# Modulation sums in operations of 1024 columns, and another address for the last FFN's first-product operand

## The chip, the cores and the metric

The kernel runs on one core of a Trainium2 chip. The metric is the device time of one execution in microseconds (us). The kernel before took 1702.43 us, the median of three runs (1701.34 to 1703.19). The profile was taken in one more execution.

## The reference

Two layers of a diffusion transformer work on 256 latent tokens and 256 context tokens of width 1024, in float32. Each layer is a feed-forward network (FFN), a mixer (window attention and retention side by side) and a second FFN. Every sublayer takes a shift, a scale and a gate from a modulation vector:

```
mod   = silu(c)     @ ada_w[l] + ada_b[l]      # 9 x 1024 numbers per layer, latent stream
mod_c = silu(c_ctx) @ ada_w[l] + ada_b[l]      # the same for the context stream

u = rmsnorm(h, g_pre) * (1 + scale) + shift    # swiglu_sublayer
a, b = split(u @ wi);  y = (silu(a) * b) @ wo
h = h + 0.5 * gate * rmsnorm(y, g_post)
```

`wi` is 1024 x 5632 and `wo` 2816 x 1024. In the last layer the context stream ends at the mixer, so the last FFN has 256 tokens where the others have 512. `ada_w[l]` is 1024 x 9216; the product with it is a matrix by one vector per stream.

## The kernel before, in words

**Products.** TensorE (PE) takes operands rounded to fp32r. Each float32 operand is split into a high part and a rest, and a product is made of three matmuls: high by high, rest by high, high by rest. In the first product of an FFN (`uT`) the weights of 128 x 128 are the stationary operand, `whi` (L203, L204) or `wlo` (L205), and the activations `uh` and `ul` move through: 512 columns (two streams of 256), in the last FFN 256 columns. In the second product and in the mixer's output product the activations are stationary and 512 columns of weights move.

**Weights.** SyncE (SP) issues the loads in one queue: 512 KB into `raw` (five buffers). ScalarE (ACT) makes `whi` (L165) and VectorE (DVE) makes `wlo = raw - whi` (L166), 128 x 1024 at a time, with three buffers each. A step of an FFN's first product, `pair(f)`, takes two such weights and 48 matmuls, after which ACT and DVE make one gated tile `g` (L438, L439).

**Modulation.** The first two of the 18 modulation vectors come from PE at the start (`ada_slice`). The other 16 are summed on DVE, beside the FFNs' products: `ada_steps` runs in eight steps per vector. A step loads two half rows of 256 KB (`rawa`, three buffers, on SP's queue with the weights) and makes four operations of 512 columns (L284), each a product with `cbc` and a sum along the row into one column of `adacc`; the elementwise result goes to `junk` and is not read. After eight steps the two half sums are added (L289, `adav`) and `ada_done` makes the shift, scale or gate. `Filler` hands these steps out between the pairs of an FFN; they are bound by `start[0]` and `behind[0]` not to come before a given load and a given VectorE operation.

**Mixer.** In the retention part, `ret_out` makes the heads' outputs in `ps_ry`; ACT copies the second half (`y2`, L840) and DVE adds it (L841), then come the statistics on DVE, a power on GpSimd (POOL), and ACT scales each 128 x 128 tile with `rgn` (L855). `ret_T` transposes four of them on PE into `ps_ro` (L861), and ACT and DVE split that into `uh` and `ul` (L874) for the output product (`ps_wo`, L213 to L215). `y2` has one buffer of its own, `yr2`.

**Order.** The program is written as one list, and a scheduler puts each engine's instructions in an order from the operations' costs and from when buffers come free; this order is fixed when the kernel is built. The engines run each its own list and wait for one another by semaphores. Most short-lived tiles come from one pool of 26 slots of 2 KB per partition (`t2k`), which are handed round in the order of the requests.

**Addresses.** In the built kernel the tiles of `uh`, `ul`, `whi`, `wlo` and `w4` all begin at addresses that leave 160 when divided by 512 bytes, and so do all slices of them that a matmul of an FFN's first product reads.

Of the kernel before, what the change touches and what calls it, by code (L numbers as in the profile page):

```python
# [15 lines left out]
P = 128  # L16
L = 2
D = 1024
# [14 lines left out]
def hybrid_kernel(ctx: ExitStack, tc: tile.TileContext, A: dict, out: bass.AP):  # L33
# [18 lines left out]
    def small(shape, name, bufs=4):  # L52
        return t2.tile(shape, F32, tag=name, name=name, bufs=bufs)
# [18 lines left out]
    shT = const.tile([P, 3, 2, KT], F32, name="shT")  # L72
    scT = const.tile([P, 3, 2, KT], F32, name="scT")
    cbc = const.tile([P, 2, D], F32, name="cbc")
    ctile = const.tile([P, KT, 32], F32, name="ctile")

    def keep_warm(n):

# [11 lines left out]

    h = act.tile([P, 4, D], F32, name="h")

    uh = act.tile([P, 2, KT, LAT], R, name="uh")
    ul = act.tile([P, 2, KT, LAT], R, name="ul")

    c_in = small([P, KT, 2], "c_in", 1)
    nc.sync.dma_start(c_in, A["cT"])
# [100 lines left out]
    def uT(ps, w2, k, s0, s1):  # L198

        ps = ps.rearrange("p (s c) -> p s c", c=LAT)  # L200
        hi, lo = (w[:, k, :] for w in w2)
        mhi, mlo = (x[:, s0:s1, k, :] for x in (uh, ul))
        nc.tensor.matmul(ps, lhsT=hi, rhs=mhi, start=(k == 0), stop=False)  # L203
        nc.tensor.matmul(ps, lhsT=hi, rhs=mlo, start=False, stop=False)  # L204
        nc.tensor.matmul(ps, lhsT=lo, rhs=mhi, start=False, stop=(k == KT - 1))  # L205
# [15 lines left out]
    def ada_done(l, m, v):  # L221

        sub, kind = divmod(m, 3)
        for st in range(2):
            b = adab[:, l, m, :]
            if kind == 0:
                nc.vector.tensor_add(shT[:, sub, st, :], v[:, st, :], b)
            elif kind == 1:
                nc.vector.tensor_add(v[:, st, :], v[:, st, :], b)
                nc.vector.scalar_tensor_tensor(out=scT[:, sub, st, :], in0=v[:, st, :], scalar=1.0,  # L230
                                               in1=gpre[:, l, sub, :], op0=ALU.add, op1=ALU.mult)
            else:
                nc.vector.tensor_add(v[:, st, :], v[:, st, :], b)
                nc.vector.scalar_tensor_tensor(out=v[:, st, :], in0=v[:, st, :], scalar=(1.0 if sub == 1 else 0.5),
                                               in1=gpost[:, l, sub, :], op0=ALU.mult, op1=ALU.mult)
        if kind == 2:
            pt = psum([2 * KT, P], "ps_mt")
            nc.tensor.transpose(pt, v.rearrange("p s k -> p (s k)"), ident)
            row = small([2 * KT, P], "grow", 1)
            nc.vector.tensor_copy(row, pt)  # L240
            gd = dram.tile([2, D], F32, name=f"gd{l}{m}", tag=f"gd{l}{m}")
            nc.gpsimd.dma_start(gd.rearrange("s (k c) -> (s k) c", c=P), row)
            gdram[l, sub] = gd

    def ada_slice(j):


        ps = psum([P, 256], "ps_ada")
        for i in range(2):
            for m in range(2):  # L250
                wr = load_raw(A["ada_w0"][j, m, i], (4, 256))
                r = 64 * m + 32 * i
                for k in range(4):
                    nc.tensor.matmul(ps[r:r + 32, :], lhsT=ctile[:, 4 * i + k, :], rhs=wr[:, k, :], start=(k == 0),
                                     stop=(k == 3))
        mod = t2k([P, 256], name="mod")
        nc.scalar.activation(mod, ps, AF.Copy)
        pt = psum([P, 2, 2, 2], "ps_mt")
        for c2 in range(2):
            nc.tensor.matmul(pt[:, c2].rearrange("p m s -> p (m s)"), lhsT=mod[:, 128 * c2:128 * c2 + 128],  # L260
                             rhs=sel.rearrange("p m s -> p (m s)"), start=True, stop=True)
        ks = slice(2 * j, 2 * j + 2)
        v = small([P, 2, KT], "adav", 1)
        for st in range(2):
            nc.vector.tensor_add(shT[:, 0, st, ks], pt[:, :, 0, st], adab[:, 0, 0, ks])
            nc.vector.tensor_add(v[:, st, ks], pt[:, :, 1, st], adab[:, 0, 1, ks])
            nc.vector.scalar_tensor_tensor(out=scT[:, 0, st, ks], in0=v[:, st, ks], scalar=1.0,
                                           in1=gpre[:, 0, 0, ks], op0=ALU.add, op1=ALU.mult)
# [3 lines left out]

    def ada_steps(l, m):

        acc = small([P, 2, 2, KT], "adacc", 2)
        for k in range(KT):
            wr = [wp.tile([P, 512], F32, tag="rawa", name="rawa", bufs=3) for _ in range(2)]
            for i in range(2):
                with tc.issue_after(start[0]):
                    nc.sync.dma_start(wr[i], A["ada_w"][l, m, k, :, 512 * i:512 * i + 512])  # L280
                with tc.issue_after(behind[0]):
                    for st in range(2):
                        junk = small([P, 512], "junk", 2)
                        nc.vector.scalar_tensor_tensor(out=junk, in0=wr[i], scalar=1.0,  # L284
                                                       in1=cbc[:, st, 512 * i:512 * i + 512], op0=ALU.mult,
                                                       op1=ALU.mult, accum_out=acc[:, i, st, k:k + 1])
            yield
        v = small([P, 2, KT], "adav", 1)
        nc.vector.tensor_add(v, acc[:, 0], acc[:, 1])  # L289
        ada_done(l, m, v)  # L290

    class Filler:
# [72 lines left out]
    def pre_norm_part(sub, s, xn, k2):  # L365
        pt = psum([P, 2, 256], "ps_tr")
        for k in (0, 1):
            q, c0 = divmod(128 * (k2 + k), 512)
            for i in (0, 1):
                last = nc.tensor.transpose(pt[:, k, 128 * i:128 * i + 128], xn[i][q][:, c0:c0 + 128], ident)  # L370
        uf = t2k([P, 2, 256], name="uf")
        for k in (0, 1):
            sc, sh = scT[:, sub, s, k2 + k:k2 + k + 1], shT[:, sub, s, k2 + k:k2 + k + 1]
            nc.scalar.activation(uf[:, k, :], pt[:, k, :], AF.Identity, scale=sc, bias=sh)
        hi = uh[:, s, k2:k2 + 2, :]
        nc.vector.tensor_copy(hi, uf)  # L376
        behind[0] = nc.vector.tensor_sub(ul[:, s, k2:k2 + 2, :], uf, hi.bitcast(F32)).ins  # L377
        return last.ins

    def post_half(y, gates, t, half, part):  # L380


        junk = small([P, 512], "junk", 2)
        ss = small([P, 1], "ssy", 12)
        nc.scalar.activation(junk, y, AF.Square, scale=D ** -0.5, accum_out=ss)
        if half:
            st = small([P, 1], "ssum", 12)
            nc.vector.scalar_tensor_tensor(out=st, in0=part[0][0], scalar=RMS_EPS, in1=ss, op0=ALU.add, op1=ALU.add)
            ss = rsqrt(st)
        x = t2k([P, 512], name="x")  # L390
        nc.vector.tensor_mul(x, y, gates[t // 2][:, 512 * half:512 * half + 512])
        part[half] = ss, x
# [37 lines left out]
    def ffn(l, name, sub, streams, fill, nxt):  # L430
# [38 lines left out]
        def first_of_all():  # L469

            for t in range(4):
                pre_scale(t)
            t2.tile([P, 64], F32, name="pad3", tag="pad3", bufs=1)
            xn = [[xns.pop(2 * s), xns.pop(2 * s + 1)] for s in range(2)]
            gf = [t2k([P, n], name="g") for _ in range(2)]
            ps = [psum([P, n], "ps_up") for _ in range(4)]

            def norm(j):
                for s in range(2):
                    pre_norm_part(0, s, xn[s], 2 * j)  # L480

            def mm(j, f):
                for i in range(2 * f, 2 * f + 2):
                    for k in (2 * j, 2 * j + 1):
                        uT(ps[i], w[i], k, 0, 2)

            ada_slice(0)
            norm(0)
            w = [load(0, 0), load(0, 1), load(1, 0), load_w_4(wi[l, 3])]
            for j in range(4):  # L490
                mm(j, 0)
                if j < 3:
                    ada_slice(j + 1)
                    norm(j + 1)
                mm(j, 1)
            for f in range(2):
                gated(gf[f], *ps[2 * f:2 * f + 2])
            g.extend(gf)
# [59 lines left out]
    def mixer(l, last):  # L558
# [271 lines left out]
        def ret_out(hd):  # L830
            for s in range(streams):
# [4 lines left out]
                        nc.tensor.matmul(py[:, i], lhsT=pp[:, 128 * i:128 * i + 128], rhs=vr[kt][:, hd],  # L836
                                         start=(n_ == 0), stop=(n_ == len(both) - 1))
                y = small([P, 2, P], "yr", 4)
                y2 = small([P, 2, P], "yr2", 1)
                nc.scalar.activation(y2, py[:, :, 1, :], AF.Copy)  # L840
                nc.vector.tensor_add(y, py[:, :, 0, :], y2)  # L841
                st = small([P, 2, 6], "bst", 4)
# [83 lines left out]
        if last:  # L926
            for t in range(nt):
                for half in range(2):
                    mm(half, 3, t)
                    post_half(ys[half, t], gates, t, half, parts[t])  # L930
                post_norm(parts[t], t, 2)
                pre_scale(t)
                fill.step(1)
            keep_warm(12)
            pre_norm(2, 0)
            return
        fill.drain()
# [97 lines left out]
```

## Time and profile before

| what | value |
|---|---|
| median of three runs | 1702.43 us |
| the profiled execution, own time | 1700.97 us |
| its span (first to last instruction) | 1699.1 us |
| TensorE's granted clock, mean | 0.998 of full speed |
| PE busy | 98% of the span |
| DVE busy | 69% |
| ACT busy | 44% |
| POOL busy | 3% |

The profiled execution lies 1.46 us below the median. Its span is 1.9 us shorter than its own time, which is what lies around the first and last instruction. A busy PE is counted from modelled ends of its matmuls, which overlap, so the rate of a stretch is read from the distances between the starts of matmuls, not from their lengths. PEld is the loading of stationary operands. "Waits" lists, for an engine and line, the idle time that one releaser ended, with the number of times and the longest; the same wait can appear for PE and for PEld.

### The profile page before, as it was taken

How to read it: one execution, taken by the hardware profiler on the slowest of the kernel's cores; microseconds unless marked ns; L12 is line 12 of the kernel's file. 1: busy time of each engine (PE TensorE's matmuls, PEld its weight loads, DVE VectorE, ACT ScalarE, POOL GpSimd, SP SyncE). 2: the span in 40 equal slices, each digit the busy share in tenths (PEclk: the TensorE clock that was granted, in tenths of full speed). 3: DMA queues.
4: the chain of work that ended last, by engine and by line, in shares of the span. 5: the costliest groups of instructions: out<-in, count | busy, mean ns of one | idle time of the engine just before them, and what ended most of it. 6: DMA issues, size and time to landing. Idle time of an engine off the chain costs nothing.

```text
span 1699.1 us, 23653 instructions
## 1 busy us (share of the span) xinstructions
PE 1671.2 (98%) x8632; PEld 1408.6 (83%) x8632; DVE 1179.5 (69%) x2625; ACT 746.8 (44%) x1299; POOL 45.8 (3%) x75
## 2 busy tenths in 40 slices
PE   8999999999999999999999999999999999989998
PEld 5788788888778788888888898888888888889996
DVE  3699895496898869982245689962347589865466
ACT  4322222355787662222234452222234578754454
POOL 1000000001000110000000000000000100000000
PEclk9999999999999999999999999999999999999999
DMA  7677775252112236672333437752334222335563
GB/s 275 225 233 249 225 236 164 87 192 88 63 51 88 74 112 216 230 232 104 99 100 98 163 123 236 236 184 91 98 100 142 76 94 81 119 136 186 183 189 113
DMA packets 89270, 254.40 MB, mean 150 GB/s; under 512 B 10560, under 2 KB 11056, under 8 KB 89024
## 3 DMA queue, kind: packets, MB, share of 16 engines
q1 hardware_dynamic: 88416, 251.16, 45.0%
q0 software_dynamic: 736, 1.72, 0.3%
q8 instruction: 68, 1.11, 0.3%
q14 instruction: 50, 0.41, 0.1%
HBM read 251.74 MB, written 1.10 MB: 149 GB/s over the span
## 4 chain that ended last, share of the span: by engine, by line
PE 80%; DVE 7%; ACT 3%; DMA 3%; issue 2%; POOL 1%; DVEq 0%; POOLq 0%; ACTq 0%
PE ps_up L203 14%; PE ps_up L205 14%; PE ps_up L204 14%; PE ps_dn L535 8%; PE ps_dn L536 8%; PE ps_dn L537 8%; DMA rawa<-in_ada_w 3%; DVE junk L284 2%; DVE wlo L166 2%; PE ps_pj L203 1%; PE ps_pj L204 1%; PE ps_pk L213 1%; PE ps_pj L205 1%; PE ps_pk L215 1%; PE ps_po L693 1%
## 5 line engine op out<-in xcount | busy, mean ns | idle before, releaser
L165 ACT ACTIVATE whi<-raw 128x1024 fp32r<-128x1024 f32 x297 | 314.7, 1060 | 769.7 <-PE ps_up L204 499.0
L166 DVE TENSOR_TENSOR wlo<-raw,whi 128x1024 fp32r<-128x1024 f32 x297 | 362.9, 1222 | 284.5 <-ACT whi L165 279.6
L203 PE MATMUL ps_up<-uh,whi 128*128 128x512 f32 (+1 forms) x1400 | 502.1, 359 | 2.5 <-DVE uh L376 2.4
L205 PE MATMUL ps_up<-uh,wlo 128*128 128x512 f32 (+1 forms) x1400 | 502.3, 359 | 2.2 <-DVE wlo L166 2.1
L204 PE MATMUL ps_up<-ul,whi 128*128 128x512 f32 (+1 forms) x1400 | 501.8, 358 | 0.0
L284 DVE SCALAR_TENSOR_TENSOR junk<-rawa,cbc 128x512 f32<-128x512 f32 x512 | 325.8, 687 | 27.0 <-DMA rawa<-in_ada_w 26.3
L205 PEld LDWEIGHTS ps_up<-uh,wlo 128*128 128x128 f32 x1400 | 265.2, 189 | 43.7 <-DVE wlo L166 5.1
L203 PEld LDWEIGHTS ps_up<-uh,whi 128*128 128x128 f32 x1400 | 264.9, 189 | 42.7 <-DVE uh L376 3.8
L204 PEld LDWEIGHTS ps_up<-ul,whi 128*128 128x128 f32 x1400 | 265.3, 189 | 39.0 <-DVE ul L377 0.8
L537 PE MATMUL ps_dn<-wlo,ghl 128*128 128x512 f32 x560 | 217.9, 389 | 0.0
L536 PE MATMUL ps_dn<-whi,ghl 128*128 128x512 f32 x560 | 217.9, 389 | 0.0
L535 PE MATMUL ps_dn<-whi,ghl 128*128 128x512 f32 x560 | 216.9, 391 | 0.2
L535 PEld LDWEIGHTS ps_dn<-whi,ghl 128*128 128x128 f32 x560 | 104.6, 188 | 24.1 <-ACT ghl L525 3.0
L536 PEld LDWEIGHTS ps_dn<-whi,ghl 128*128 128x128 f32 x560 | 105.1, 188 | 22.3 <-DVE ghl L526 0.4
L537 PEld LDWEIGHTS ps_dn<-wlo,ghl 128*128 128x128 f32 x560 | 105.1, 188 | 21.9
L439 DVE TENSOR_TENSOR g<-g,ps_up 128x512 f32<-128x512 f32 (+1 forms) x92 | 55.0, 598 | 85.9 <-PE ps_up L205 79.7
L526 DVE TENSOR_TENSOR ghl<-g,ghl 128x512 fp32r<-128x512 f32 (+1 forms) x176 | 102.8, 619 | 1.4 <-ACT ghl L525 1.0
L525 ACT ACTIVATE ghl<-g 128x512 fp32r<-128x512 f32 (+1 forms) x176 | 92.1, 564 | 24.8 <-DVE g L439 15.9
L203 PE MATMUL ps_pj<-uh,whi 128*128 128x256 f32 (+1 forms) x168 | 58.7, 349 | 0.0
L204 PE MATMUL ps_pj<-ul,whi 128*128 128x256 f32 (+1 forms) x168 | 56.0, 333 | 0.1
L205 PE MATMUL ps_pj<-uh,wlo 128*128 128x256 f32 (+1 forms) x168 | 55.6, 331 | 0.0
L438 ACT ACTIVATE g<-ps_up 128x512 f32<-128x512 f32 (+1 forms) x92 | 47.0, 511 | 0.0
(220 smaller groups left out, 1958.9 us busy)
## 6 DMA issues: line engine op xcount, KB each, us to landing
raw<-in_ffn_wi SPq DMA_DIRECT2D x176, 512.0 KB, 3.8
rawa<-in_ada_w SPq DMA_DIRECT2D x256, 256.0 KB, 3.3
raw<-in_ffn_wo SPq DMA_DIRECT2D x88, 512.0 KB, 3.4
raw<-in_w_in SPq DMA_DIRECT2D x20, 512.0 KB, 3.4
raw<-in_ada_w SPq DMA_DIRECT2D x16, 512.0 KB, 5.7
raw<-in_w_in_t SPq DMA_DIRECT2D x16, 512.0 KB, 3.3
raw<-in_w_out SPq DMA_DIRECT2D x16, 512.0 KB, 3.5
gate<-gd SPq DMA_DIRECT2D x10, 512.0 KB, 4.2
```

What stands on the lines that cost most here:

```text
L165: nc.scalar.activation(hi, raw, AF.Copy)
L166: nc.vector.tensor_sub(lo, raw, hi.bitcast(F32))
L203: nc.tensor.matmul(ps, lhsT=hi, rhs=mhi, start=(k == 0), stop=False)
L204: nc.tensor.matmul(ps, lhsT=hi, rhs=mlo, start=False, stop=False)
L205: nc.tensor.matmul(ps, lhsT=lo, rhs=mhi, start=False, stop=(k == KT - 1))
L284: nc.vector.scalar_tensor_tensor(out=junk, in0=wr[i], scalar=1.0, in1=cbc[:, st, 512 * i:512 * i + 512], op0=ALU.mult, op1=ALU.mult, accum ...
L439: nc.vector.tensor_mul(gs, gs, b)
L525: nc.scalar.activation(g2[0][i], g[2 * c + i], AF.Copy)
L526: nc.vector.tensor_sub(g2[1][i], g[2 * c + i], g2[0][i].bitcast(F32))
L535: nc.tensor.matmul(y, lhsT=ghi[i][:, cs], rhs=hi[i], start=(f == 0), stop=False)
L536: nc.tensor.matmul(y, lhsT=glo[i][:, cs], rhs=hi[i], start=False, stop=False)
L537: last = nc.tensor.matmul(y, lhsT=ghi[i][:, cs], rhs=lo[i], start=False, stop=(f == NFF - 1))
```

## The change

Three things are changed.

1. `ada_steps` loads one whole row of 512 KB per step (two buffers of 4 KB per partition instead of three of 2 KB) and makes two operations of 1024 columns instead of four of 512. The sums go straight into `adav`, which now has two buffers; `adacc` and the addition at L289 are gone. The unread result goes to `junka`, one buffer of 4 KB.
2. Tiles that had room of their own are taken from the `t2k` pool, which keeps its 26 slots: `ctile`, `grow`, the `junk` of `post_half`, and `y2` of `ret_out` (the buffer `yr2`).
3. The tiles of `uh` and `ul` are 128 floats longer. Before the last `pre_norm`, which writes the operand of the last FFN's first product, `uu` is set to views that begin 48 floats (192 bytes) further on. `uT` reads through `uu`. In the built kernel the moving operand of these matmuls then leaves 352 when divided by 512, and the weights 160 as before. `u_tok`, `split_u` and `load_w_u` keep the old views.

```
-    ctile = const.tile([P, KT, 32], F32, name="ctile")
+    ctile = t2k([P, KT, 32], name="ctile")
...
-    uh = act.tile([P, 2, KT, LAT], R, name="uh")
-    ul = act.tile([P, 2, KT, LAT], R, name="ul")
+    SHIFT = 48
+    uhs, uls = (act.tile([P, 2 * KT * LAT + 128], R, name=n) for n in ("uh", "ul"))
+    u_at = lambda x, o: x[:, o:o + 2 * KT * LAT].rearrange("p (s k c) -> p s k c", s=2, k=KT)
+    uh, ul = u_at(uhs, 0), u_at(uls, 0)
+
+    uu = [uh, ul]
...
-        mhi, mlo = (x[:, s0:s1, k, :] for x in (uh, ul))
+        mhi, mlo = (x[:, s0:s1, k, :] for x in uu)
...
-            row = small([2 * KT, P], "grow", 1)
+            row = t2k([2 * KT, P], name="grow")
...
-        v = small([P, 2, KT], "adav", 1)
+        v = small([P, 2, KT], "adav", 2)
...
-        acc = small([P, 2, 2, KT], "adacc", 2)
+        v = small([P, 2, KT], "adav", 2)
         for k in range(KT):
-            wr = [wp.tile([P, 512], F32, tag="rawa", name="rawa", bufs=3) for _ in range(2)]
-            for i in range(2):
-                with tc.issue_after(start[0]):
-                    nc.sync.dma_start(wr[i], A["ada_w"][l, m, k, :, 512 * i:512 * i + 512])
-                with tc.issue_after(behind[0]):
-                    for st in range(2):
-                        junk = small([P, 512], "junk", 2)
-                        nc.vector.scalar_tensor_tensor(out=junk, in0=wr[i], scalar=1.0,
-                                                       in1=cbc[:, st, 512 * i:512 * i + 512], op0=ALU.mult,
-                                                       op1=ALU.mult, accum_out=acc[:, i, st, k:k + 1])
+            wr = wp.tile([P, D], F32, tag="rawa", name="rawa", bufs=2)
+            with tc.issue_after(start[0]):
+                nc.sync.dma_start(wr, A["ada_w"][l, m, k])
+            with tc.issue_after(behind[0]):
+                for st in range(2):
+                    junk = small([P, D], "junka", 1)
+                    nc.vector.scalar_tensor_tensor(out=junk, in0=wr, scalar=1.0, in1=cbc[:, st, :], op0=ALU.mult,
+                                                   op1=ALU.mult, accum_out=v[:, st, k:k + 1])
             yield
-        v = small([P, 2, KT], "adav", 1)
-        nc.vector.tensor_add(v, acc[:, 0], acc[:, 1])
         ada_done(l, m, v)
...
-        hi = uh[:, s, k2:k2 + 2, :]
+        hi = uu[0][:, s, k2:k2 + 2, :]
...
-        junk = small([P, 512], "junk", 2)
+        junk = t2k([P, 512], name="junk")
...
-                y2 = small([P, 2, P], "yr2", 1)
+                y2 = t2k([P, 2, P], name="yr2")
...
             keep_warm(12)
+            uu[:] = u_at(uhs, SHIFT), u_at(uls, SHIFT)
             pre_norm(2, 0)
```

Lines of the changed kernel from L76 on are a few numbers higher: L166 is L170 there, L284 is L287, L213 is L217; L439, L840, L855 and L861 are the same.

The order of the instructions moves at two places. On DVE in the first FFN, two pairs of the first product stood like this before (a pair ends with `g`; `wlo` is a weight's rest, `rawa` a row of modulation weights):

```order
L284 SCALAR_TENSOR_TENSOR junk,adacc<-rawa,cbc 128x512 x5
L166 TENSOR_TENSOR wlo<-raw,whi 128x1024
L284 SCALAR_TENSOR_TENSOR junk,adacc<-rawa,cbc 128x512 x6
L439 TENSOR_TENSOR g<-g,ps_up 128x512
L284 SCALAR_TENSOR_TENSOR junk,adacc<-rawa,cbc 128x512
L166 TENSOR_TENSOR wlo<-raw,whi 128x1024
L284 SCALAR_TENSOR_TENSOR junk,adacc<-rawa,cbc 128x512 x5
L166 TENSOR_TENSOR wlo<-raw,whi 128x1024
L284 SCALAR_TENSOR_TENSOR junk,adacc<-rawa,cbc 128x512 x6
L439 TENSOR_TENSOR g<-g,ps_up 128x512
```

and stand like this now:

```order
L170 TENSOR_TENSOR wlo<-raw,whi 128x1024
L287 SCALAR_TENSOR_TENSOR junka,adav<-rawa,cbc 128x1024 x3
L170 TENSOR_TENSOR wlo<-raw,whi 128x1024
L287 SCALAR_TENSOR_TENSOR junka,adav<-rawa,cbc 128x1024 x3
L439 TENSOR_TENSOR g<-g,ps_up 128x512
L170 TENSOR_TENSOR wlo<-raw,whi 128x1024
L287 SCALAR_TENSOR_TENSOR junka,adav<-rawa,cbc 128x1024 x3
L170 TENSOR_TENSOR wlo<-raw,whi 128x1024
L287 SCALAR_TENSOR_TENSOR junka,adav<-rawa,cbc 128x1024 x3
L439 TENSOR_TENSOR g<-g,ps_up 128x512
L170 TENSOR_TENSOR wlo<-raw,whi 128x1024
```

Twelve operations of 512 columns per pair have become six of 1024, in two strings of three, each between one `wlo` and what follows it.

On ACT in the first layer's mixer, the end of the retention part stood like this before (`yr_` with a number is the copy `y2`, `yr<-yr,rgn` the scaling, `uh<-ps_ro` the first step after the transposes):

```order
L840 ACTIVATE yr_5684<-ps_ry 128x256
L874 ACTIVATE uh<-ps_ro 128x2x256
L165 ACTIVATE whi<-raw 128x1024
L823 ACTIVATE pmh<-pm 128x512 x2
L840 ACTIVATE yr_5749<-ps_ry 128x256
L191 ACTIVATE wt<-raw 128x512
L165 ACTIVATE whi<-raw 128x1024
L855 ACTIVATE yr<-yr,rgn 128x128 x2
L840 ACTIVATE yr_5775<-ps_ry 128x256
L191 ACTIVATE wt<-raw 128x512
L874 ACTIVATE uh<-ps_ro 128x2x256
```

and stands like this now:

```order
L823 ACTIVATE pmh<-pm 128x512
L840 ACTIVATE yr_5308<-ps_ry 128x256
L840 ACTIVATE yr_5334<-ps_ry 128x256
L840 ACTIVATE yr_5399<-ps_ry 128x256
L840 ACTIVATE yr_5425<-ps_ry 128x256
L169 ACTIVATE whi<-raw 128x1024
L855 ACTIVATE yr<-yr,rgn 128x128 x2
L195 ACTIVATE wt<-raw 128x512
L855 ACTIVATE yr<-yr,rgn 128x128 x2
L169 ACTIVATE whi<-raw 128x1024
L855 ACTIVATE yr<-yr,rgn 128x128 x2
L874 ACTIVATE uh<-ps_ro 128x2x256
```

With its own single buffer a copy could not be placed before the addition that read the one before it. Now four copies stand in a row, ahead of a weight's high part and of all six scalings, and the scalings stand with weights of the output product between them.

## Rows read from the trace of the kernel before

**Rows 1.** The page, part 1: busy time, share of the span, instructions.

```profile
PE 1671.2 (98%) x8632; PEld 1408.6 (83%) x8632; DVE 1179.5 (69%) x2625; ACT 746.8 (44%) x1299; POOL 45.8 (3%) x75
```

**Rows 2.** The page, part 4: the chain that ended last, by line.

```profile
PE ps_up L203 14%; PE ps_up L205 14%; PE ps_up L204 14%; PE ps_dn L535 8%; PE ps_dn L536 8%; PE ps_dn L537 8%; DMA rawa<-in_ada_w 3%; DVE junk L284 2%; DVE wlo L166 2%; PE ps_pj L203 1%; PE ps_pj L204 1%; PE ps_pk L213 1%; PE ps_pj L205 1%; PE ps_pk L215 1%; PE ps_po L693 1%
```

**Rows 3.** Stretches: us from:to, busy (instructions), clock, DMA share, GB/s.

```profile
100.00:200.00 100.00, 98.26 (x430) 80.01 (x429) 89.28 (x245) 23.46 (x27) 0.57 (x1) 1.00 0.73 232
...
1400.00:1500.00 100.00, 97.13 (x542) 81.09 (x540) 89.47 (x206) 76.31 (x150) 4.61 (x7) 1.00 0.31 102
1510.00:1630.00 120.00, 120.00 (x1002) 120.00 (x1002) 60.19 (x66) 51.16 (x67) 0.00 (x0) 1.00 0.55 180
```

**Rows 4.** Waits of 100 to 300 us: us in total, times, longest us.

```profile
DVE junk L284 <- DMA rawa<-in_ada_w: 13.4, 17, 1.8
...
PEld ps_up L205 <- DVE wlo L166: 5.1, 7, 1.3
PE ps_up L205 <- DVE wlo L166: 2.1, 4, 0.9
```

**Rows 5.** DVE's timeline from 160.9 us: start, length, instruction.

```profile
161.55 1.22 DVE L166 TENSOR_TENSOR wlo<-raw,whi 128x1024 fp32r<-128x1024 f32 x1
162.69 0.69 DVE L284 SCALAR_TENSOR_TENSOR junk<-rawa,cbc 128x512 f32<-128x512 f32 x1
...
163.30 0.69 DVE L284 SCALAR_TENSOR_TENSOR junk<-rawa,cbc 128x512 f32<-128x512 f32 x1
...
165.75 0.08 DVE L284 DVE_READ_ACCUMULATOR junk<-rawa,cbc 128x1 f32 x1
165.87 0.17 DVE L289 TENSOR_TENSOR adav<-adacc 128x16 f32<-128x16 f32 x1
```

**Rows 6.** DMA issues, 100 to 300 us: count, KB each, us to landing.

```profile
rawa<-in_ada_w SPq DMA_DIRECT2D x86, 256.0 KB, 3.4
raw<-in_ffn_wi SPq DMA_DIRECT2D x27, 512.0 KB, 4.0
```

**Rows 7.** Waits of 540 to 610 us (first layer's retention).

```profile
PEld ps_ro L861 <- ACT yr L855: 3.7, 4, 2.0
```

**Rows 8.** Waits of 1440 to 1505 us (last layer's retention).

```profile
PEld ps_tr L370 <- DVE xn L355: 4.6, 1, 4.6
...
PEld ps_ro L861 <- ACT yr L855: 1.3, 2, 0.7
```

**Rows 9.** PE's timeline from 1492 us: moving operand of 512 columns.

```profile
1492.00 0.39 PE L215 MATMUL ps_wo<-wlo,uh 128*128 128x512 f32 x1
...
1494.72 0.40 PE L215 MATMUL ps_wo<-wt,uh 128*128 128x512 f32 x1
```

**Rows 10.** PE's timeline from 1549.7 us: the last FFN's first product.

```profile
1549.78 0.28 PE L205 MATMUL ps_up<-uh,wlo 128*128 128x256 f32 x1
...
1551.46 0.28 PE L204 MATMUL ps_up<-ul,whi 128*128 128x256 f32 x1
```

**Rows 11.** PE's timeline from 1378.8 us: 256 columns in the mixer's projection.

```profile
1378.87 0.28 PE L205 MATMUL ps_pj<-uh,wlo 128*128 128x256 f32 x1
...
1379.45 0.28 PE L204 MATMUL ps_pj<-ul,whi 128*128 128x256 f32 x1
```

**Rows 12.** PE's timeline from 622.1 us: a product's first two matmuls.

```profile
622.17 0.28 PE L203 MATMUL ps_up<-uh,whi 128*128 128x256 f32 x1
622.28 0.28 PE L204 MATMUL ps_up<-ul,whi 128*128 128x256 f32 x1
```

**Rows 13.** Weight loads by line, 1510 to 1630 us: count, busy us, mean ns.

```profile
L204 PEld LDWEIGHTS ps_up<-ul,whi 128*128 128x128 f32 x319 | 61.2, 192 | 0.0
```

**Rows 14.** Weight loads of the second product, the page, part 5.

```profile
L535 PEld LDWEIGHTS ps_dn<-whi,ghl 128*128 128x128 f32 x560 | 104.6, 188 | 24.1 <-ACT ghl L525 3.0
```

**Rows 15.** PE's timeline from 438.1 us: 512 columns beside other work.

```profile
438.19 0.40 PE L203 MATMUL ps_pj<-uh,whi 128*128 128x512 f32 x1
438.43 0.39 PE L204 MATMUL ps_pj<-ul,whi 128*128 128x512 f32 x1
```

More of the change, by code (lines that the diff above doesn't have):

```diff
@@ L374, in pre_norm_part @@
             nc.scalar.activation(uf[:, k, :], pt[:, k, :], AF.Identity, scale=sc, bias=sh)
-        hi = uh[:, s, k2:k2 + 2, :]
+        hi = uu[0][:, s, k2:k2 + 2, :]
         nc.vector.tensor_copy(hi, uf)
-        behind[0] = nc.vector.tensor_sub(ul[:, s, k2:k2 + 2, :], uf, hi.bitcast(F32)).ins
+        behind[0] = nc.vector.tensor_sub(uu[1][:, s, k2:k2 + 2, :], uf, hi.bitcast(F32)).ins
         return last.ins
     def post_half(y, gates, t, half, part):
-        junk = small([P, 512], "junk", 2)
+        junk = t2k([P, 512], name="junk")
         ss = small([P, 1], "ssy", 12)
@@ L472, in first_of_all @@
                 pre_scale(t)
-            t2.tile([P, 64], F32, name="pad3", tag="pad3", bufs=1)
+            t2.tile([P, 48], F32, name="pad3", tag="pad3", bufs=1)
             xn = [[xns.pop(2 * s), xns.pop(2 * s + 1)] for s in range(2)]
```

## The prediction

> **What bounds the kernel now.** I read the page's busy times, then the chain of waits, then busy times by stretch, then the waits inside the stretches the change touches, and last the starts of single instructions. PE is busy for 1671.2 us of the 1699.1 us span, DVE for 69% [rows 1]. The chain that ended last is mostly the FFNs' products, with three entries of modulation work in it: the load of `rawa` 3%, the sums 2%, `wlo` 2% [rows 2]. So PE sets the end, and two things can change the time: PE's waits, of which the span has at most 1699.1 − 1671.2 = 27.9 us, and the rate of its matmuls. Three stretches matter [rows 3]. In 100 to 200 us, the first FFN with the modulation sums, DVE is 89.28% busy and PE waits 1.74 us in a hundred. In 1400 to 1500 us, the last retention part, DVE is 89.47% busy and PE waits 2.87 us. In 1510 to 1630 us, the last FFN's first product, PE never waits and DVE is half idle. All run at a granted clock of 1.00, so what follows is at 2.4 GHz.
>
> **Modulation sums.** Of the 18 vectors 16 are summed on DVE, 8 steps each, 128 steps. 256 loads of 256 KB become 128 of 512 KB, and 512 operations of 512 columns become 256 of 1024. Does DVE gain? Operations of 512 columns follow each other 0.61 us apart (162.69 to 163.30), with a read of the accumulator of 0.08 that lies under the next operation [rows 5]. The trace has no sum of 1024 columns; its nearest row is `wlo`, 1024 columns, behind which the next operation starts 1.14 us later [rows 5]. Two of 512 take 1.22 us, so the bare gain would be 0.08 per operation, 256 × 0.08 = 20 us of DVE time over the kernel. But all write into one `junka`, and before two `junk` buffers took turns. If an operation must wait for the read behind the one before it, the chain is 1.14 + 0.08 for the read + 0.04 (which `adav` at 165.87 started after the read that began at 165.75) = 1.26 us against 1.22. I count DVE's work as unchanged.
>
> What PE sees depends on DVE's order. A pair of the first FFN takes 48 matmuls × 0.227 (12 steps in 2.72 us [rows 9], the same form of 512 columns) = 10.9 us. DVE has in it 12 × 0.61 + 2 × 1.14 + 0.6 (the gated product, near the 0.61 of a 512-column operation) = 10.2 us, 0.7 below PE, both before and after. The sums now stand in strings of three, 3.8 us each, between two `wlo`; before it was five or six of 512, 3.1 to 3.7 us. A string that waits for its row keeps the next `wlo` waiting, then `ps_up` L205, and with it all of PE. In 100 to 300 us DVE waits 13.4 us for `rawa`, 17 times, and of this PE's weight loads feel 5.1 us in 7 waits behind `wlo`; the 2.1 us at PE are the same waits seen at the matmul [rows 4].
>
> The row buffers turn more slowly. A buffer was in use for 2 × 0.61 = 1.22 us and empty for the landing, 3.4 us for 256 KB [rows 6]; with three of them six half rows take 6 × 4.62 / 3 = 9.2 us of the 10.9. A whole row is in use for 2.5 us, and 512 KB landed in 4.0 us as `raw` on the same queue [rows 6]; with two buffers three rows take 3 × 6.5 / 2 = 9.8 us. It still fits, with 1.1 us to spare where there was 1.7. The added `adav` buffer and the missing additions (16 × 0.17 [rows 5] = 2.7 us of DVE) lie beside PE's products.
>
> Price: each of the 7 waits that PE feels becomes longer by the 0.6 us by which a row lands later, 4.2 us; or PE waits once more what it waited at the matmuls, 2.1 us. I take the middle, **+3 us**. Below, all 5.1 us can vanish, as rows come in half the number of loads: −5.1. Above, all that DVE waits for rows reaches PE: 13.4 − 5.1 = +8.3.
>
> **The tiles taken from the pool.** `ctile`, `grow` and `post_half`'s `junk` are written and read within a few operations and stand where they stood; I cost them at nothing, hidden under DVE's and ACT's idle time beside the FFNs, and if one had to wait for a slot it is inside this part's upper bound. `y2` moves work. With its single buffer a copy alternated with the scaling of earlier heads; now four copies stand ahead of a weight's `whi` and of six scalings on ACT, and those scalings are mixed with weights of the output product. Behind the scalings PE's transposes into `ps_ro` are waiting: 3.7 us in four waits in the first layer [rows 7], 1.3 in two in the last [rows 8]. Work that feeds the statistics earlier also makes DVE busier early, at 89%. I expect the transposes to wait later and longer: the first layer's wait once more, 3.7, and 0.3 in the last, where the wait of 4.6 us at `ps_tr` on the chain behind it [rows 8] is not moved. **+4 us**. Bounds: both layers' waits and that one again, 3.7 + 1.3 + 4.6 = +9.6, or all gone, −9.6.
>
> **The operand's address.** 22 × 2 weights × 8 × 3 = 1056 matmuls of 256 columns read `uh` and `ul` 192 bytes further. They start 0.120 us apart (14 steps in 1.68 us [rows 10]), 1056 × 0.120 = 126.7 us, and nothing but PE sets this stretch. With 512 columns it is 0.227, so 256 columns more cost 0.107; 256 columns at that rate alone are 0.107 and 0.013 are a fixed part. No row shows another address. But the same form has run faster: 0.58 us for 5 steps, 0.117, in the projection [rows 11], and 0.11 once at a product's start [rows 12]. So the 0.120 is not the floor, and something beside the columns, such as the weight load that goes on meanwhile, holds it. I take the row with several steps, 0.117: 1056 × 0.003 = **−3.2 us**. Below, the whole fixed part goes: 1056 × 0.0132 = −13.9. Above, operands that lie badly to each other: matmuls of 512 columns beside other work stood 0.24 apart where 0.227 is steady [rows 15], 0.013 more, +13.7.
>
> A weight load beside these products takes 192 ns [rows 13]; beside the second product of the FFNs, with 512 moving columns, 188 ns [rows 14]. So the two reads seem to touch each other a little. The Trainium skill ("TensorE: Matmul & The Clock Gate", "Step-by-step: what each phase is for", on LDWEIGHTS) says that the next weights come in by a read port of their own and take nothing from the running matmul. By that rule the address changes nothing, this term is 0 and the sum +7, as in rival C; the 4 ns speak a little against it, and no run here settles it.
>
> **Sum.** 3 + 4 − 3.2 = +3.8 us on the profiled execution's own 1700.97, 1704.8. That execution lies 1.46 below the median of the runs, so **1706 us** against 1702.43.
>
> **Rivals.** A: the address matters more than the order. The pitch falls to between 0.113 (−7.4) and 0.107 (−13.9) and the kernel is faster in spite of +7: 1702.43 + 7 − 7.4 = 1702 down to 1695.5. For it: the 0.11 [rows 12]; a stretch of 126.7 us in which only PE's rate counts. Against it: that pitch is seen only where PE had just changed its product, never in a steady run. It wins from 0.1134 on, where 1056 × 0.0066 = 7 us.
> B: the order costs nothing, since DVE's slack of 0.7 us per pair and ACT's idle 24% in the retention stretch [rows 3] take it up. Then only −3.2 is left: 1699. Against it: DVE at 89% in both stretches.
> C: the address does nothing: 1702.43 + 7 = 1709.4.
> D: rows come too late. Each pair needs two `wlo` behind strings of whole rows, and the 1.1 us of slack in the buffers' turn is used up from the point where a row lands over 0.7 us later than 4.0 (3 × 7.2 / 2 = 10.8). Then modulation costs +8.3 or more: 1711 to 1716. Against it: the DMA engines are 73% busy there [rows 3], with as many bytes as before.
>
> **Chances.** About 0.2%, 3.4 us, is what a measurement of this kernel tells from no change: faster means below 1699.0, slower above 1705.8. The forecast has 0.34 (0.24 slower, 0.10 same); A 0.27 (0.19 faster, 0.08 same); B 0.16 (0.09 faster, 0.07 same); C 0.14 (0.13 slower, 0.01 same); D 0.09 (0.08 slower, 0.01 same). Together: faster 0.28, same 0.27, slower 0.45. The forecast's own range is 1702 to 1710. The range of 1695 to 1715 takes in A's end, C and most of D; the ends of the bounds all on one side are left out.
>
> **What would show it.** In the profile after, the starts of the last FFN's first product: 0.117 apart by the forecast, 0.113 or less by A, 0.120 by C. The waits of `ps_up` L209 (L205 before) on `wlo` in 100 to 300 us: about 8 us at the weight loads, none by B, over 13 by D; the landing of a row of 512 KB near 4.0 us. Sums of 1024 columns 1.22 to 1.26 us apart in a string; at 1.14 they don't wait for the read and DVE is freer than I count. The waits of `ps_ro` in the first mixer: 7 us or more; if they shrink, my reading of ACT's order is wrong. The forecast is wrong if the two order terms together are below 3 or above 11, or if the last FFN's pitch lies outside 0.115 to 0.120.

## The result and the profile after

The changed kernel takes 1713.40 us, the median of four runs (1710.37 to 1716.73), where the kernel before took 1702.81 in its runs beside them. The ratio is 1.0067 with a 95% interval of 1.0055 to 1.0080: slower, by 10.6 us between the medians where the forecast had 3.6. The time lies on the forecast side and inside the wide range of 1695 to 1715, but outside the forecast's own range of 1702 to 1710. The sum had the three parts the right way round and each of them too small. The profiled execution takes 1714.24 us, its span is 1712.3. One more line differs between the kernels than the change names: the unused tile `pad3` has 48 floats instead of 64; no run takes that apart.

The page of the changed kernel, parts 1 and 4 (they answer to [rows 1] and [rows 2]):

```profile
PE 1671.6 (98%) x8632; PEld 1401.6 (82%) x8632; DVE 1169.1 (68%) x2097; ACT 746.1 (44%) x1299; POOL 45.4 (3%) x75
...
PE 67%; DVE 14%; DMA 9%; issue 5%; ACT 4%; POOL 1%; SPq 0%; DVEq 0%; POOLq 0%; ACTq 0%
PE ps_up L209 10%; PE ps_up L207 10%; PE ps_up L208 10%; DMA rawa<-in_ada_w 8%; PE ps_dn L535 7%; PE ps_dn L536 7%; PE ps_dn L537 7%; DVE junka L287 6%; DVE wlo L170 3%; PE ps_pk L217 1%; PE ps_pk L219 1%; PE ps_po L693 1%; PE ps_pk L218 1%; PE ps_ada L258 1%; PE ps_pj L207 1%
```

PE has as much work as before. What grew is the modulation on the chain that ended last: the row loads from 3 to 8%, the sums from 2 to 6%.

Waits of the changed kernel, first from 100 to 306 us (first FFN, [rows 4]), then from 998 to 1242 us (the second layer's first FFN), last from 1450 to 1525 us (the last retention part, [rows 8]); total us, times, longest:

```profile
DVE junka L287 <- DMA rawa<-in_ada_w: 14.8, 21, 1.8
PEld ps_up L209 <- DVE wlo L170: 10.6, 13, 2.1
...
PE ps_up L209 <- DVE wlo L170: 4.9, 7, 1.7
...
PEld ps_up L209 <- DVE wlo L170: 5.5, 6, 2.2
PE ps_up L209 <- DVE wlo L170: 3.2, 4, 1.8
...
PEld ps_ro L861 <- ACT yr L855: 4.1, 4, 2.7
PEld ps_tr L370 <- DVE xn L355: 3.8, 1, 3.8
...
PEld ps_tr L370 <- issue: 1.7, 1, 1.7
```

PE's weight loads wait 10.6 us for `wlo` where they waited 5.1. In the last retention part `ps_ro` waits 4.1 us instead of 1.3.

Busy time by stretch of the changed kernel: the first two answer to [rows 3], the next three are the end of the last retention part, the last one lies in the last FFN's first product (the bracket behind PE counts its matmuls, the number before the DMA share is the granted clock):

```profile
100.00:200.00 100.00, 97.86 (x427) 79.17 (x425) 89.88 (x153) 22.67 (x27) 0.57 (x1) 1.00 0.75 240
200.00:300.00 100.00, 96.82 (x419) 77.65 (x418) 85.05 (x133) 24.76 (x30) 0.49 (x1) 1.00 0.70 223
...
1486.00:1494.00 8.00, 4.91 (x27) 3.71 (x26) 5.78 (x16) 4.42 (x9) 1.86 (x1) 0.98 0.39 129
1494.00:1504.00 10.00, 9.52 (x44) 7.75 (x43) 7.43 (x20) 5.39 (x11) 0.73 (x1) 0.85 0.19 58
...
1524.00:1532.00 8.00, 8.00 (x57) 7.95 (x56) 6.09 (x10) 2.87 (x7) 0.00 (x0) 0.77 0.23 73
...
1540.00:1620.00 80.00, 80.00 (x709) 80.00 (x708) 42.94 (x47) 36.13 (x47) 0.00 (x0) 1.00 0.56 188
```

Around 1490 us PE stands idle for 3.1 of 8 us, and the granted clock of the next ten is 0.85, an average of full (2.4 GHz) and half (1.2 GHz). In the last line 709 matmuls stand in 80 us; before it was 669. Their starts are 113.3 ns apart, not 120.

Where the time went, in stages that I worked out from the starts of PE's instructions in each profile. "First product" runs from its first matmul to the first of the second product; "retention" from the first `ps_ry` to the first matmul of the next FFN. All in us; other stages differ by 1 us at most.

| profile | first FFN, first product | retention, layer 1 | layer 2's first FFN | retention, layer 2 | last FFN, first product |
|---|---|---|---|---|---|
| before | 265.6 | 65.8 | 242.5 | 43.5 | 127.6 |
| changed | 271.5 | 67.7 | 247.2 | 50.1 | 121.5 |
| e1, address alone | 262.5 | 65.8 | 242.5 | 44.0 | 125.6 |
| e12, the same again | 263.6 | 65.8 | 242.5 | 43.8 | 121.2 |
| e3, changed without address | 270.6 | 67.7 | 242.5 | 50.1 | 128.4 |
| e5, y2 in the pool alone | 268.1 | 67.7 | 242.5 | 50.0 | 128.4 |
| e6, sums | 272.7 | 65.9 | 243.8 | 42.9 | 126.9 |
| e7, three row buffers | 261.2 | 67.7 | 242.5 | 50.1 | 128.2 |
| e9, without the two losses | 261.4 | 65.8 | 242.5 | 43.2 | 121.0 |

Each row is one execution. Between the first two rows: 5.9 + 1.9 + 4.7 + 6.6 − 6.1 = 13.0 of the 13.2 us between the spans.

### The profile page after: what moved, and what is told of

The parts are those of the page before. It is cut to its first block, busy times and chain, and to the rows that moved or that the text cites. A ratio compares the mean times of both kernels' runs of the same rounds, so it can differ in the third digit from the quotient of the medians.

```text
span 1712.3 us, 22775 instructions
## 1 busy us (share of the span) xinstructions
PE 1671.6 (98%) x8632; PEld 1401.6 (82%) x8632; DVE 1169.1 (68%) x2097; ACT 746.1 (44%) x1299; POOL 45.4 (3%) x75
## 4 chain that ended last, share of the span: by engine, by line
PE 67%; DVE 14%; DMA 9%; issue 5%; ACT 4%; POOL 1%; SPq 0%; DVEq 0%; POOLq 0%; ACTq 0%
PE ps_up L209 10%; PE ps_up L207 10%; PE ps_up L208 10%; DMA rawa<-in_ada_w 8%; PE ps_dn L535 7%; PE ps_dn L536 7%; PE ps_dn L537 7%; DVE junka L287 6%; DVE wlo L170 3%; PE ps_pk L217 1%; PE ps_pk L219 1%; PE ps_po L693 1%; PE ps_pk L218 1%; PE ps_ada L258 1%; PE ps_pj L207 1%
## 5 line engine op out<-in xcount | busy, mean ns | idle before, releaser
L170 DVE TENSOR_TENSOR wlo<-raw,whi 128x1024 fp32r<-128x1024 f32 x297 | 362.6, 1222 | 298.8 <-ACT whi L169 296.9
L287 DVE SCALAR_TENSOR_TENSOR junka<-rawa,cbc 128x1024 f32<-128x1024 f32 x256 | 313.2, 1223 | 41.6 <-DMA rawa<-in_ada_w 36.8
L439 DVE TENSOR_TENSOR g<-g,ps_up 128x512 f32<-128x512 f32 (+1 forms) x92 | 55.0, 598 | 72.1 <-PE ps_up L209 68.0
```

The lines of the kernel that those rows point to most:

```text
L170: nc.vector.tensor_sub(lo, raw, hi.bitcast(F32))
L287: nc.vector.scalar_tensor_tensor(out=junk, in0=wr, scalar=1.0, in1=cbc[:, st, :], op0=ALU.mult, op1=ALU.mult, accum_out=v[:, st, k:k + 1])
L439: nc.vector.tensor_mul(gs, gs, b)
```

## The experiments

Three parts are to be told apart: a loss by the sums' row buffers, a loss by the order of the retention part, and a gain by the address. Each is undone or made alone.

**e1, the address alone** (on the kernel before; e12 is the same file).

```
+    uhs, uls = (act.tile([P, 2 * KT * LAT + 128], R, name=n) for n in ("uh", "ul"))
...
+            uu[:] = u_at(uhs, SHIFT), u_at(uls, SHIFT)      # SHIFT = 48
```

> The kernel before with only the operand of the last FFN's first product moved by 192 bytes; the order of every engine's list is as before. Theory (the address sets the distance of these matmuls): the 1056 matmuls start 113.3 ns apart instead of 120, 7.1 us less, near 1695.7 us, and nothing else moves. Rival (the distance came down with the other parts of the change, for example by what DVE and the DMAs do meanwhile): 120 ns and 1702 to 1703 us.

Measured: 1692.38 us against 1699.07, ratio 0.9966 (0.9953 to 0.9978), a gain of 6.7 us. Its times run from 1689.9 to 1700.3, wider than before's (1697.3 to 1700.6). The profile had a distance of 117.8 ns (the 117.6 in the next expectation is this one), neither of the two numbers expected.

> The kernel with the address alone once more, one profile. Its first profile had 117.6 ns in the whole of the last FFN's first product, the changed kernel with the same addresses 113.3. Theory (how the weight loads and the products stand to each other when the stretch begins decides the rate, anew in each execution): another rate than 117.6 can come, 113.3 in the whole stretch, and a time near 1690. Rival (something in this kernel fixes it, such as where other tiles lie): 117.6 ns again.

Measured: 113.3 ns, 1692.84 us against 1698.10. The two profiles of one kernel, the stretch of 1540 to 1620 us, e1 and then e12:

```profile
1540.00:1620.00 80.00, 80.00 (x682) 80.00 (x681) 40.19 (x42) 34.12 (x43) 0.00 (x0) 1.00 0.55 185
```

```profile
1540.00:1620.00 80.00, 80.00 (x709) 80.00 (x708) 41.86 (x44) 35.91 (x45) 0.00 (x0) 1.00 0.57 193
```

With the same addresses and the same order 682 matmuls in one execution, 709 in the other. So the program alone does not fix the rate, and each execution held its own through the stretch. The two executions ran on different chips, but e2 below, on the chip of e1, had 113.3. The 117.8 looks like a mixture, (2 × 120.0 + 113.3) / 3, and in that profile the weight loads of one of the three products take 192 ns and the others 188. What decides it stays open.

**e4, 512 bytes; e8, e10, e11, e2: 256, 64, 128 and 192 bytes in every product.**

```
+    uh, ul = u_at(uhs, SHIFT), u_at(uls, SHIFT)             # SHIFT = 64, 16, 32, 48
```

> The kernel before with the operand of the last FFN's first product moved by 512 bytes, which leaves 160 modulo 512 as before. Theory (the remainder by 512 counts): 120 ns apart and no change, 1701 to 1704 us. Rival (any other place helps, for example because the operand no longer lies where an earlier stage wrote): 113 ns and near 1695.7 us.

> The kernel before with uh and ul 192 bytes further in every product, not in the last FFN alone, so that the 512-column matmuls of the other FFNs and of the mixer's projection also have their moving operand at 352 and their weights at 160 modulo 512. Theory (the address takes 6.7 ns from every such matmul whatever its length): 3192 matmuls of 512 columns at 220 instead of 227 ns and 1824 of 256 at 113.3, together 3192 x 6.7 + 1824 x 6.7 = 33 us less, near 1669 us where no other engine becomes the bound. Rival (only the short matmuls gain, since 512 columns leave room beside the next weight load): 512 columns stay at 227 ns, 1824 x 6.7 = 12 us less, near 1691 us.

> The kernel before with uh and ul 256 bytes further in every product, 416 against 160 modulo 512. With 192 bytes the 512-column matmuls went from 227 up to 231 and 236 ns and the 256-column ones from 120 down to 113. Theory (the distance counts the way a half period would): 256 bytes is the farthest, both lengths at their shortest, 113 and 220 ns, near 1670 us. Rival (512 columns lose with any offset): 230 ns or more for 512, 113 to 118 for 256, 1705 to 1712 us.

> The kernel before with uh and ul 64 bytes further in every product, 224 against 160 modulo 512. 256 bytes gave what no offset gave (120 and 227 ns), so the remainder by 256 may be what counts, and 192 is then 64 on the other side. Theory (the side matters): 64 bytes does the opposite, 256 columns slower than 120 ns and 512 columns below 227. Rival (only the distance matters): as with 192, 113 to 118 ns for 256 columns and 230 to 236 for 512, near 1710 us.

> The kernel before with uh and ul 128 bytes further in every product, 288 against 160 modulo 512. Theory (a period of 256 bytes, of which 128 is the middle): both lengths differ most from no offset, 256 columns at 113 ns and 512 at 231 to 236 or more. Rival (the period is 128 bytes or less): 120 and 227 ns, no change.

Measured (distance of starts in ns, for 512 columns the middle half of them; in e4 only the last FFN is moved; the times of all but e2, which has four, are of one execution):

| bytes | 256 columns, last FFN | 512 columns, other FFNs | time, us | before beside it |
|---|---|---|---|---|
| 0 (before) | 120 | 226 to 227 | | |
| 64 (e10) | 117 to 119 | 226 to 231 | 1704.65 | 1699.61 |
| 128 (e11) | 115 to 122 | 229 to 237 | 1717.56 | 1699.61 |
| 192 (e2) | 113 to 114 | 231 to 236 | 1709.65 | 1699.07 |
| 256 (e8) | 120 | 226 to 227 | 1700.00 | 1700.53 |
| 512 (e4) | 120 | 226 to 227 | 1698.51 | 1699.07 |

For 512 columns, the stretch of 700 to 800 us in e4, e2 and e8, in this order:

```profile
700.00:800.00 100.00, 100.00 (x443) 82.81 (x442) 68.00 (x160) 23.84 (x28) 0.00 (x0) 1.00 0.56 185
```

```profile
700.00:800.00 100.00, 100.00 (x430) 80.60 (x429) 69.82 (x173) 22.94 (x27) 0.00 (x0) 1.00 0.58 194
```

```profile
700.00:800.00 100.00, 100.00 (x443) 82.84 (x442) 69.31 (x164) 24.03 (x28) 0.00 (x0) 1.00 0.56 188
```

My theory for e2 was wrong by sign: 430 instead of 443 matmuls, ratio 1.0067 (1.0052 to 1.0082). The first products of the three 512-token FFNs take 268.4, 247.7 and 248.5 us, 5 to 6 more each than in e4. 256 and 512 bytes do nothing, so among the offsets tried the remainder by 256 counts. Neither of the plain rules in my expectations holds for 512 columns: 64 bytes is not the same as 192 (medians 229 and 233 ns), nor its opposite, and the middle, 128, is no best. For 256 columns e10's 117.8 is also what e1 had with 192 bytes, so one execution cannot tell the two offsets apart. Only products of 256 columns gain.

The same profiles hold products with the roles turned round. In the mixers' output product (`ps_wo`) the activations are the stationary operand, so the offset moves the stationary address and the moving weights stay. Medians of the distances there, beside those of the first products of 512 columns, where the activations move:

| bytes | activations move (`ps_up`) | activations stationary (`ps_wo`) |
|---|---|---|
| 0 (before) | 227 | 227 |
| 64 (e10) | 229 | 234 |
| 128 (e11) | 232 | 232 |
| 192 (e2) | 233 | 229 |
| 256 (e8) | 227 | 227 |

What 64 bytes do on one side, 192 do on the other, and 64 + 192 = 256. So in these profiles, one of each kernel, the difference of the two addresses counts, with its sign, and not the place of the moving operand by itself.

**e3, the changed kernel without the offset** (`SHIFT = 0`).

> The changed kernel with the operand where it was before (160 modulo 512); order as in the changed kernel. Theory (three parts that add up): 120 ns in the last FFN's first product, 7.1 us above the changed kernel's median of 1713.4, near 1720.5 us; the first and second first-FFN and both retention stretches lose the same 6, 5, 2 and 7 us. Rival (the waits before the last FFN take up part of it): 1713 to 1717 us.

Measured: 1714.85 us against 1699.07, ratio 1.0095 (1.0079 to 1.0112). So the rest of the change costs 15.8 us. On the 1702.81 of the first measurement that ratio is 1719.0, near the theory and above the rival. The distance was 120 ns, as expected. The loss in layer 2's first FFN did not come back here (242.5): it is not in every execution.

**e5, y2 in the pool alone** (on the kernel before).

```
-                y2 = small([P, 2, P], "yr2", 1)
+                y2 = t2k([P, 2, P], name="yr2")
```

> The kernel before with y2 alone taken from the 26 slots; modulation, address and the other tiles as before. Theory (the order of the retention part costs what it cost in the changed kernel): the first layer's retention to the next FFN takes 67.7 us instead of 65.9, the last layer's 50 instead of 43.8, together 8 us more, ratio near 1.005. Rival (the order is harmless by itself and was late only because modulation left other work there): no change within 2 us.

Measured: 1709.86 against 1700.53, ratio 1.0061 (1.0040 to 1.0081). Both retention stretches are as in the changed kernel, 67.7 and 50.0, though the sums are untouched. The rival is out: this order costs by itself. Waits in e5, 1440 to 1520 us:

```profile
PEld ps_ro L861 <- ACT yr L855: 4.1, 4, 2.7
PE ps_ro L861 <- ACT yr L855: 2.7, 2, 2.2
PEld ps_wo L213 <- ACT whi L165: 1.2, 1, 1.2
```

The same 4.1 us in four waits, the longest 2.7, that the changed kernel has.

**e6, the sums** (the changed kernel with `SHIFT = 0`, y2 in its own buffer, 25 slots).

> The changed kernel with the address of before and with y2 in its own single buffer again, for which the pool has 25 slots; what is left is the sums of 1024 columns with two row buffers and the three small tiles in the pool. Theory: the retention stretches are back at 65.9 and 43.8 us, and the modulation costs 5 to 11 us, in the first FFNs of the layers, ratio 1.003 to 1.0065. Rival (all of the loss is the order in the mixers): within 2 us of before. The prediction had +3 for this part.

Measured: 1706.28 against 1700.53, ratio 1.0041 (1.0026 to 1.0056). The retention stretches are back at 65.9 and 42.9; the first FFN takes 272.7. The 5.8 us here and the 9.3 of e5 make 15.1 of the 15.8 in e3, so the two losses add up.

**e7, three row buffers** (the changed kernel with `SHIFT = 0`, 24 slots).

```
-            wr = wp.tile([P, D], F32, tag="rawa", name="rawa", bufs=2)
+            wr = wp.tile([P, D], F32, tag="rawa", name="rawa", bufs=3)
```

> The changed kernel with the address of before and three row buffers of 4 KB instead of two, for which the pool has 24 slots; the order in the retention part is that of the changed kernel. Theory (DVE waits for rows since two buffers turn too slowly, and wlo stands behind): DVE's waits for rawa fall by half or more, the first FFN comes back from 271 to 265 us or less, and the kernel is 5 to 8 us below the one with two buffers, ratio 1.004 to 1.006 to before. Rival (the strings of three sums delay wlo whatever the buffers): the waits of ps_up on wlo stay, ratio near 1.0095.

Measured: 1706.73 against 1700.53, ratio 1.0041 (1.0027 to 1.0055), with the retention loss of e5 still in it. In 100 to 300 us there is no wait for `rawa` and none for `wlo` at PE any more. The stretch of 100 to 200 us in e6 and then in e7:

```profile
100.00:200.00 100.00, 96.70 (x424) 78.49 (x423) 89.93 (x151) 22.41 (x26) 0.57 (x1) 1.00 0.72 237
```

```profile
100.00:200.00 100.00, 100.00 (x443) 82.70 (x442) 98.72 (x161) 23.48 (x27) 0.57 (x1) 1.00 0.77 261
```

DVE goes to 98.72% and PE is never idle. The long operations and the strings of three harm nothing by themselves; with two buffers PE waits, with three (and 24 slots instead of 26) it does not.

**e9, without the two losses**: the changed kernel with three row buffers, y2 in its own buffer, 24 slots, and tiles longer by 64 floats instead of 128, which puts `ul` 256 bytes off `uh`.

> The sums of 1024 columns with three row buffers of 4 KB, y2 in its own single buffer, 24 slots in the pool, and the last FFN's operand 192 bytes further (the tiles of uh and ul longer by 64 floats). Theory (the parts add up once the two losses are gone): first FFN 261 us as with three buffers (before 263 to 266), retention stretches 65.9 and 43.5, the last FFN's first product at 113 to 118 ns instead of 120, 2 to 7 us less; together 6 to 10 us below before, ratio 0.994 to 0.9965. Rival (with 24 slots other work comes late): no better than the address alone, 0.9966 or above.

Measured: 1690.65 us (1689.69 to 1691.75) against 1699.61, ratio 0.9947 (0.9935 to 0.9959): 9.0 us faster than the kernel before, and so faster than the changed one. The first FFN and the last are at the best of the table. Against e1 (0.9953 to 0.9978) the intervals overlap, so no run shows that the larger sums, with three buffers, pay anything beside the address.

## Why the prediction was right, and where its steps failed

The side and the wide range came out; by its own signs the forecast failed. It called itself wrong if the two order terms together were above 11 us, and they are 15.8 in e3, or if the last FFN's distance lay below 0.115 us, and it is 0.1133. Of the other signs, the weight loads' waits for `wlo` (10.6 us) lie between its 8 and rival D's 13, and those of `ps_ro` in the first mixer (3.9 us) did not reach its 7.

**Modulation, +3: right by sign, too small.** The first FFN takes 270.6 to 272.7 us with two row buffers (three profiles) and 262.5 to 268.1 in six with the old sums and 227 ns: about 7 us. Layer 2's first FFN adds 0, 1.3 or 4.7 by execution. DVE's chain was right: in the changed kernel the sums of one string stand 1.27 us apart (forecast 1.26).

```profile
229.47 1.23 DVE L287 SCALAR_TENSOR_TENSOR junka<-rawa,cbc 128x1024 f32<-128x1024 f32 x1 [0.66 <-DMA rawa<-in_ada_w]
230.62 0.08 DVE L287 DVE_READ_ACCUMULATOR junka<-rawa,cbc 128x1 f32 x1
230.74 1.22 DVE L287 SCALAR_TENSOR_TENSOR junka<-rawa,cbc 128x1024 f32<-128x1024 f32 x1
231.89 0.08 DVE L287 DVE_READ_ACCUMULATOR junka<-rawa,cbc 128x1 f32 x1
232.35 1.22 DVE L287 SCALAR_TENSOR_TENSOR junka<-rawa,cbc 128x1024 f32<-128x1024 f32 x1 [0.38 <-DMA rawa<-in_ada_w]
```

The step that failed is "It still fits, with 1.1 us to spare". The prediction had a row land in 4.0 us and hold its buffer for 2.5. In the lines above the first row is used until 231.97. SP's queue issues the next load into its buffer at 232.00, and `g` stands between the two sums of the second row:

```profile
232.00 3.69 SPq L283 DMA_DIRECT2D rawa<-in_ada_w  x2
...
233.51 0.68 DVE L439 TENSOR_TENSOR g<-g,ps_up 128x512 f32<-128x512 f32 x1
234.11 1.22 DVE L287 SCALAR_TENSOR_TENSOR junka<-rawa,cbc 128x1024 f32<-128x1024 f32 x1
```

Around 205 us the chain that ended last goes through a buffer whose row is held longer still (start, us, what):

```profile
204.47 4.79 DMA rawa<-in_ada_w
...
211.19 1.14 DVE wlo L170
212.33 1.01 DVE junka L287
213.50 4.49 DMA rawa<-in_ada_w
```

The next load follows the last use at once. But of the 50 rows loaded from 100 to 300 us the median lands after 4.3 us, not 4.0, and strings of three sums cut rows in two: where `g`, `wlo` or both stand between a row's two sums, as in 14 of the 50, the buffer is held 4.1 us (median) instead of 2.5. The prediction had the strings and counted every row as whole. Three loads in turn, from one issue into a buffer to the next, took 7.05 + 9.03 + 7.04 us from 201.9 us on, and 7.24 + 7.66 + 6.91 from 224.8 on: by two buffers 11.6 and 10.9 us, where I had 9.8 and PE gives 10.9. So the 1.1 us were gone. In effect that is rival D, rows come too late, which I gave 0.09; but its condition, a row that lands 0.7 us later than 4.0, was not met, as the landing was 0.3 late and the held rows did the rest. e7 shows it from the other side: a third buffer takes all these waits away.

**Retention, +4: right by sign, half the size, the cause right in part.** e5 gives 9.3 us by its medians, and 1.9 + 6.5 by the stages. In the last layer the turn I named happens: `ps_ro` waits longer, 4.1 against 1.3 at the weight loads, and at the matmuls (1440 to 1505 us before, 1450 to 1525 in the changed kernel):

```profile
PE ps_ro L861 <- ACT yr L855: 0.5, 2, 0.3
...
PE ps_ro L861 <- ACT yr L855: 2.7, 2, 2.2
```

These 2.2 us are a third of the 6.5. What I had not priced is the clock: after PE's idle time near 1490 us the next ten run at 0.85, 1.5 us of PE time. All four profiles with `y2` in the pool (changed, e3, e5, e7) have 3.4 us at half speed some 30 us before the last FFN begins, and none of the ten others has. The last FFN then begins at half speed for 15 matmuls (213 ns apart) where it was 6 before; but with `y2` in its own buffer that number goes from 0 to 12 by execution, so not all of it belongs to the order. In the first layer the weight loads' wait at `ps_ro` is 3.9 us, in seven pieces (540 to 615 us), against 3.7; at the matmuls it even fell, from 2.3 to 1.8, while `ps_wo` waits 1.2 us for `uh`, which it did not before. The rest of the 1.9 there is not explained. That I expected 3.7 of the 4 there was wrong: it is the last layer that pays.

**Address, −3.2: right by sign, half the size.** The distance fell to 113.3 ns in the changed kernel, 1056 × 6.7 = 7.1 us, of which the slow start took back about 1: 127.6 − 121.5 = 6.1. That is nearer to the 0.11 of a product's first two matmuls [rows 12], which I had set aside for the row with several steps [rows 11]. Rival A's mechanism is real; it did not decide, as the two orders cost 16 and not 7 us.

The Trainium skill's rule ("TensorE: Matmul & The Clock Gate", "Step-by-step: what each phase is for", on LDWEIGHTS), that loading the next weights takes nothing from the running matmul, doesn't hold here as it stands: e1, e2 and e11 change an address alone, and both lengths of product change their rate; by the table with the roles turned round, it is the address of the one read against that of the other that counts. No run has these products without a weight load beside them. The loads changed with it, 188 ns in the changed kernel (lines of PEld, 1535 to 1620 us) against 192 [rows 13]:

```profile
L209 PEld LDWEIGHTS ps_up<-uh,wlo 128*128 128x128 f32 x245 | 46.0, 188 | 0.0
```

Beside 512 columns they take 188 ns with and without the offset (e2 and before, 700 to 800 us), though those products go from 227 to 233.

**Sum.** 16 − 6 instead of 7 − 3.2: the forecast of 1706 is 7.4 us low, and the errors of the first two terms were partly covered by that of the third. That this kept the time inside the wide range is luck: without the gain by the address, e3 stands near 1719. Rival B (the order costs nothing) is refuted by e5 and e6, C (no effect of the address) by e1.

## What to carry to other kernels

Count a buffer's turn with everything in it: the landing, the wait in the consumer's list, and the whole time from the first use to the last, with the other work that the list puts between; then see whether buffers × the consumer's period cover the turns of all that one period needs, before making transfers larger and buffers fewer. A scratch tile with a single buffer also holds an order in place; moving it to a pool lets a scheduler run work ahead of what the critical engine waits for. An offset between moving operand and weights is worth trying for each product length by itself, and needs several executions, since one kernel can run at two rates.

## What the runs showed of the hardware

The address of the moving against that of the stationary operand, modulo 256 bytes among the five offsets tried, moves the distance of fp32r matmuls: 113 to 122 ns for 256 columns, 226 to 237 for 512. The offset of 192 bytes, the best for 256 columns, is bad for 512. One address gave 117.8 and 113.3 ns in two executions of the same kernel, each held for 120 us.

In the changed kernel PE stood idle for 3.1 us between 1486 and 1494 us, and from 1493.6 its granted clock was half (1.2 GHz) for 3.4 us. The three other kernels with that order have the same stretch.
